# Block one's two attentions: one written-out order for TensorE, ACT and DVE, with grouped-query scores two pairs a step and weight splits two at a time

## The chip, the cores and the metric

The kernel runs on one core of a Trainium2 chip. The metric is the device time in microseconds (us) of one execution. TensorE (PE in the rows) does the matmuls and transposes; ACT (ScalarE), DVE (VectorE) and POOL (GpSimd) work beside it; SP (SyncE) issues the loads. Matmul results land in PSUM banks, from which ACT and DVE read them.

## The reference, cut to what matters

Two transformer blocks on x of 256 x 1024, all in float32. The change touches the first: its projections, two attentions, and the output projection. The feed-forward part of it, and the whole second block, follow.

```python
h = rmsnorm(x, attn_norm_g)
qa, ka, va, qb, kb, vb = split(h @ w_in)        # 512, 128, 128, 512, 512, 512 columns
# A: grouped-query, 8 query heads on 2 key/value heads of 64, rotary positions
qa, ka = rope(rmsnorm(qa, a_q_norm_g)), rope(rmsnorm(ka, a_k_norm_g))
out_a = softmax(qa @ ka.T * 64**-0.5) @ va
# B: differential, 4 heads, each with two query/key parts of 64 and values of 128
qb, kb = rmsnorm(qb, b_q_norm_g), rmsnorm(kb, b_k_norm_g)
p = softmax(qb @ kb.T * 64**-0.5 + rel_bias[t5_bucket(k_pos - q_pos)])   # for each part c = 0, 1
ob = (p[c=0] - lam * p[c=1]) @ vb
out_b = rmsnorm(ob, b_subln_g) * (1 - 0.2)
x = x + concat(out_a, out_b) @ w_out
u = relu(rmsnorm(x, mlp_norm_g) @ w_up) ** 2
x = x + u @ w_down
x = second_block(x, c, ...)                     # modulation c @ w_ada_2, two gated FFNs, two mixers
```

## The kernel before

**Products and their weights.** A float32 product is made of three matmuls on values split in a high and a low half (`block`, L265 to L267: high x high, high x low, low x high). The 256 rows are two tiles of 128, the index `t` (or `qt` for queries). Half a chunk of 512 output columns is one *block*: 12 matmuls of 128 x 512. Weights come through the class `Stream`: pieces of 512 KB are loaded by SP into a ring of seven `raw` buffers and split into `hi` and `lo` in a ring of six, or in places of their own (`wbig`, `wph`). One split is an ACT copy (L137) and a DVE subtraction (L138). `split_to(i)` writes the splits up to item `i` into the program; `need` does so for the items a chunk is about to read. Between the weights stand the pieces of `w_ada_2`, of which DVE makes the second block's modulation (`mod`, L487).

**Generators as filler.** `chunk` projects 512 columns: for each `t` half the blocks, a `yield`, the other half, then its evacuation. The evacuations of `kb` and `qb` (`ev_b`) are a head norm (ACT square, DVE reduction L456, ACT logarithm and exp, three DVE steps L251 to L253, the multiply L466 into `kn`), four transposes (L727), and an ACT copy into `kbT` or `qbT` (L728); transposes are put in the list `later`, which the next `flush()` empties. `vb` is copied by ACT (L735). The list `filler` holds these generators, and `fill(n)` runs n steps of it. `wout_q(t, kh)` is the output projection, one generator for each query tile and each attention (`kh` 0 is A, 1 is B).

**The attentions.** `gqa()` (A) and `diff()` (B) each return three stages. A unit of A is (`qt`, `jp`, `g`), a pair of query heads on one key head; at `g` 0 it issues the scores of both `g` into two `aux` banks. Its DVE work is a maximum (L769) and its product with the norm (L771), its ACT work two exps (L774), its ratio a reciprocal (L778). A unit of B is (`qt`, `hp`): eight matmuls (L827) into two `aux` banks, the bias added on DVE (L834), maxima (L838), four exps on ACT (L841), then reciprocal and combination on DVE (L844 to L849) into `s`. Stage two transposes (L785, L856) and copies the result to `eT` or `aT`; stage three multiplies with the values (L798, and its like for B) and, with the last unit of a query tile, normalises into `oa` or `ob` and transposes that to the operand `MX` of the output projection (`to_hl`, L389). There are three `acc`, four `aux` and one `flex` PSUM banks.

**What sets the order.** The units are interleaved by `ga_[:6] + df_[:3] + ga_[6:7] + df_[3:] + ga_[7:]`; each loop step runs the three stages of three neighbouring units and one `fill()`. PE runs in the order in which the code issues (`manual_schedule` for PE); the order of ACT and DVE in the same stretch is chosen by the tile scheduler. SP issues loads as ring buffers come free.

Of the kernel before, what the change touches and what calls it, by code (L numbers as in the profile page):

```python
# [15 lines left out]
ALU = mybir.AluOpType  # L16
# [4 lines left out]
P = 128  # L21
# [143 lines left out]
def body(ctx: ExitStack, tc: tile.TileContext, a: dict, out: bass.AP):  # L165
# [120 lines left out]
    def chunk(xv, items, n, evac, ahead=4):  # L286

        st.need(items)
        for t in range(2):
            ps = acc()  # L290
            if t == 0:
                st.split_to(items[-1] + 1 + ahead)
            half = (len(items) + 1) // 2
            block(ps, *xv, 0, items[:half], t, n, True, False)
            yield
            block(ps, *xv, 2 * half, items[half:], t, n, False, True)
            flush()
            evac(t, ps)
            yield
# [440 lines left out]

# [9 lines left out]
    def gqa():  # L750
        pv, rec, ex, exT, sc2 = {}, {}, {}, {}, {}

        def scores(u):
            qt, jp, g = u
            if jp == g == 0:
                rec[qt] = small(8, "rec")
            if g == 0:

                for w in range(2):
                    sc2[w] = aux()  # L760
                for i in range(2):
                    for w in range(2):
                        nc.tensor.matmul(
                            sc2[w][:, i * S : (i + 1) * S], qaT[w * 64 : (w + 1) * 64, 2 * jp + i, qt * P : (qt + 1) * P],
                            kaT[w * 64 : (w + 1) * 64, :], start=True, stop=True,
                        )
            ps = sc2.pop(g)
            nm, sm = small(2, "nm"), small(2, "sm")
            nc.vector.tensor_reduce(nm, ps.rearrange("p (g k) -> p g k", g=2), AX, ALU.max, negate=True)  # L769
            h = 4 * g + 2 * jp  # L770
            nc.vector.tensor_tensor(nm, nm, rq[:, qt, h : h + 2], ALU.mult)  # L771
            e = s512("e")
            for i in range(2):
                nc.scalar.activation(  # L774
                    e[:, i * S : (i + 1) * S], ps[:, i * S : (i + 1) * S], AF.Exp, bias=nm[:, i : i + 1],
                    scale=rq[:, qt, h + i : h + i + 1], accum_out=sm[:, i : i + 1],
                )
            nc.vector.reciprocal(rec[qt][:, h : h + 2], sm)  # L778
            ex[u] = e

        def trans(u):
            e = ex.pop(u)
            p2 = aux()
            for b in range(4):
                nc.tensor.transpose(p2[:, b * P : (b + 1) * P], e[:, b * P : (b + 1) * P], ident)  # L785
            eT = s512("eT")
            nc.scalar.activation(eT, p2, AF.Copy)
            exT[u] = eT

        def pvs(u):  # L790
            qt, jp, g = u
            if jp == g == 0:
                pv[qt] = acc()
            eT = exT.pop(u)
            for i in range(2):
                h = 4 * g + 2 * jp + i
                for kt in range(2):
                    nc.tensor.matmul(  # L798
                        pv[qt][:, h * 64 : (h + 1) * 64], eT[:, (2 * i + kt) * P : (2 * i + kt + 1) * P], va[:, kt, g * 64 : (g + 1) * 64],
                        start=kt == 0, stop=kt == 1,  # L800
                    )
            if jp == g == 1:
                oa = s512("oa")
                nc.vector.tensor_tensor(
                    oa.rearrange("p (h d) -> p h d", d=64), pv[qt].rearrange("p (h d) -> p h d", d=64),
                    rec[qt].unsqueeze(2).to_broadcast([P, 8, 64]), ALU.mult,
                )
                fill()
                to_hl(oa, MX, 0, qt)

        return scores, trans, pvs

    def diff():
        pv, at, atT, rec = {}, {}, {}, {}

        def scores(u):
            qt, hp = u
            flex_free[0] = False
            if hp == 0:
                rec[qt] = small(8, "recb")  # L820
            s = []
            nm, sm, rr = small(4, "nm"), small(4, "sm"), small(4, "rr")
# [8 lines left out]
            for c in range(2):  # L831
                ps = pss[c]
                s.append(s512("s"))
                nc.vector.tensor_tensor(  # L834
                    s[c].rearrange("p (h k) -> p h k", h=2), ps.rearrange("p (h k) -> p h k", h=2),
# [3 lines left out]
                for i in range(2):  # L839
# [3 lines left out]
                    )  # L843
            nc.vector.reciprocal(rr[:, 2:4], sm[:, 2:4])  # L844
# [4 lines left out]
            nc.vector.scalar_tensor_tensor(rec[qt][:, 2 * hp : 2 * hp + 2], sm[:, 0:2], EPS, sm[:, 0:2], ALU.mult, ALU.mult)  # L849
            at[u] = s[0]  # L850

        def trans(u):
            att = at.pop(u)
# [5 lines left out]
            atT[u] = aT  # L859

        def pvs(u):
            qt, hp = u
            if hp == 0:
                pv[qt] = bank("flex", 1)
            aT = atT.pop(u)
            for i in range(2):
                h = 2 * hp + i
                for kt in range(2):
                    nc.tensor.matmul(
                        pv[qt][:, h * P : (h + 1) * P], aT[:, (2 * i + kt) * P : (2 * i + kt + 1) * P], vb[:, kt, h * P : (h + 1) * P],  # L870
                        start=kt == 0, stop=kt == 1,
                    )
            if hp == 1:
                ob = s512("ob")
                head_norm(pv[qt], 4, P, ob, each=rec[qt])
# [649 lines left out]
```

## Time and profile before

| | |
|---|---|
| time, median of 3 runs | 1037.38 us (1036.73 to 1038.09) |
| the profiled execution: its time, its span | 1038.07 us, 1036.3 us |
| mean granted clock of PE over the span | 0.984 |
| PE busy | 997.0 us, 96% of the span, 5825 instructions |
| DVE busy | 724.8 us, 70% |
| ACT busy | 509.8 us, 49% |
| POOL busy | 23.2 us, 2% |
| DMA engines busy, of 16 | 61.9% (loads) |

Busy times are sums over one engine's instructions; the granted clock is the share of full speed that PE was allowed, 1.0 being 2.4 GHz and 0.5 being 1.2 GHz. A start in a row counts from the start of the span. A name such as `aux` or `kn` is a buffer of the program, `out<-in` what an instruction writes and reads.

### The profile page before, as it was taken

The numbers are of one execution on the slowest core, as the hardware profiler recorded it, in microseconds if no ns is written. First come the engines' busy times: TensorE is split into PE (matmuls) and PEld (weight loads), VectorE is DVE, ScalarE is ACT, GpSimd is POOL, SyncE is SP. The second block draws the span as 40 slices with busy tenths as digits, with TensorE's granted clock in tenths as the row PEclk, the third lists the DMA queues.
The fourth block names the chain that finished last, engine by engine and source line by source line (L and its number), as shares of the span: only waits on it lengthen the run. The fifth ranks groups of instructions, "written<-read, shape, count | busy, mean of one in ns | idle before, by whom it ended". The sixth has DMA issues, their size and how long they took to land.

```text
span 1036.3 us, 15123 instructions
## 1 busy us (share of the span) xinstructions
PE 997.0 (96%) x5825; PEld 863.0 (83%) x5825; DVE 724.8 (70%) x1006; ACT 509.8 (49%) x779; POOL 23.2 (2%) x38
## 2 busy tenths in 40 slices
PE   8788779999999999999999999999999989999998
PEld 7666567999888799998878987888887869999987
DVE  7857355789776577777855969977678776666652
ACT  6556245655455345444625566444373445444540
POOL 1000000000000100000010000000010000000000
PEclk8988899999999999999999999999999999999999
DMA  9745025788988188869924656766456636774741
GB/s 313 229 149 184 1 82 184 220 294 299 319 272 276 34 285 256 267 212 351 341 104 143 203 167 183 251 206 220 133 183 223 212 114 208 244 236 138 260 155 40
DMA packets 104714, 212.22 MB, mean 205 GB/s; under 512 B 7934, under 2 KB 15034, under 8 KB 104643
## 3 DMA queue, kind: packets, MB, share of 16 engines
q1 hardware_dynamic: 104642, 211.27, 61.9%
q8 instruction: 45, 0.74, 0.3%
q14 instruction: 27, 0.21, 0.1%
HBM read 209.14 MB, written 2.10 MB: 204 GB/s over the span
## 4 chain that ended last, share of the span: by engine, by line
PE 65%; issue 18%; DVE 2%; ACT 1%; POOL 0%; DVEq 0%; ACTq 0%; POOLq 0%
PE acc L265 9%; PE acc L267 9%; PE acc L266 9%; PE acc L325 7%; PE acc L327 7%; PE acc L326 7%; PE flex L267 3%; PE flex L265 3%; PE flex L266 3%; PE flex L325 2%; PE flex L326 2%; PE flex L327 2%; PE aux L389 1%; DVE lo L138 1%; PE aux L497 0%
## 5 line engine op out<-in xcount | busy, mean ns | idle before, releaser
L138 DVE TENSOR_TENSOR lo<-raw,hi 128x1024 fp32r<-128x1024 f32 (+1 forms) x297 | 349.2, 1185 | 121.7 <-ACT hi L137 120.3
L137 ACT ACTIVATE hi<-raw 128x1024 fp32r<-128x1024 f32 (+1 forms) x297 | 302.9, 1028 | 162.1 <-PE acc L267 69.9
L325 PE MATMUL acc<-X,hi 128*128 128x256 f32 x624 | 176.2, 282 | 0.0
L327 PE MATMUL acc<-X,hi 128*128 128x256 f32 x624 | 175.7, 282 | 0.0
L326 PE MATMUL acc<-X,lo 128*128 128x256 f32 x624 | 175.4, 281 | 0.0
L265 PE MATMUL acc<-hi,X 128*128 128x512 f32 (+1 forms) x336 | 135.1, 404 | 3.4 <-ACT X L393 1.2
L267 PE MATMUL acc<-hi,X 128*128 128x512 f32 (+1 forms) x336 | 132.7, 396 | 0.9 <-DVE X L394 0.9
L266 PE MATMUL acc<-lo,X 128*128 128x512 f32 (+1 forms) x336 | 132.9, 397 | 0.2 <-DVE lo L138 0.2
L325 PEld LDWEIGHTS acc<-X,hi 128*128 128x128 f32 x624 | 118.3, 190 | 0.3
L326 PEld LDWEIGHTS acc<-X,lo 128*128 128x128 f32 x624 | 118.2, 189 | 0.2
L327 PEld LDWEIGHTS acc<-X,hi 128*128 128x128 f32 x624 | 118.2, 189 | 0.1
L487 DVE SCALAR_TENSOR_TENSOR mod<-raw,sc,mod 128x1024 f32<-128x1024 f32 x72 | 91.9, 1277 | 0.1
L265 PEld LDWEIGHTS acc<-hi,X 128*128 128x128 f32 x336 | 64.7, 193 | 18.6 <-ACT X L393 2.6
L267 PEld LDWEIGHTS acc<-hi,X 128*128 128x128 f32 x336 | 64.7, 193 | 14.9 <-DVE X L394 1.7
L266 PEld LDWEIGHTS acc<-lo,X 128*128 128x128 f32 x336 | 64.7, 193 | 13.0 <-DVE lo L138 0.4
L267 PE MATMUL acc<-hi,U 128*128 128x512 f32 x174 | 68.5, 394 | 0.0
L266 PE MATMUL acc<-lo,U 128*128 128x512 f32 x174 | 68.3, 394 | 0.0
L265 PE MATMUL acc<-hi,U 128*128 128x512 f32 x174 | 68.1, 393 | 0.0
L325 PE MATMUL flex<-X,hi 128*128 128x256 f32 x208 | 58.7, 282 | 0.0
L327 PE MATMUL flex<-X,hi 128*128 128x256 f32 x208 | 58.5, 281 | 0.0
L326 PE MATMUL flex<-X,lo 128*128 128x256 f32 x208 | 58.5, 281 | 0.0
L325 PEld LDWEIGHTS flex<-X,hi 128*128 128x128 f32 x208 | 39.4, 190 | 0.1
(423 smaller groups left out, 1607.2 us busy)
## 6 DMA issues: line engine op xcount, KB each, us to landing
raw<-in_ffn_w_in_dram SPq DMA_DIRECT2D x80, 512.0 KB, 4.8
raw<-in_w_ada_dram SPq DMA_DIRECT2D x72, 512.0 KB, 5.3
raw<-in_w_mix_dram SPq DMA_DIRECT2D x64, 512.0 KB, 4.8
raw<-in_ffn_w_out_dram SPq DMA_DIRECT2D x44, 512.0 KB, 5.1
raw<-in_w_up_dram SPq DMA_DIRECT2D x32, 512.0 KB, 5.2
raw<-in_w_down_dram SPq DMA_DIRECT2D x32, 512.0 KB, 4.8
raw<-in_w_in_dram SPq DMA_DIRECT2D x16, 512.0 KB, 6.2
raw<-in_w_out_dram SPq DMA_DIRECT2D x16, 512.0 KB, 4.7
```

Of the source, the lines that this page charges most:

```text
L137: nc.scalar.activation(hi[:, :, :n], r[:, :, :n], AF.Copy)
L138: l = getattr(nc, eng).tensor_tensor(lo[:, :, :n], r[:, :, :n], hi[:, :, :n].bitcast(F32), ALU.subtract)
L265: nc.tensor.matmul(ps[:, c0:n], h, hi[:, j, c0:n], start=f, stop=False)
L266: nc.tensor.matmul(ps[:, c0:n], h, lo[:, j, c0:n], start=False, stop=False)
L267: nc.tensor.matmul(ps[:, c0:n], l, hi[:, j, c0:n], start=False, stop=z)
L325: nc.tensor.matmul(ps, h, xh, start=first, stop=False, skip_group_check=True)
L326: nc.tensor.matmul(ps, l, xh, start=False, stop=False, skip_group_check=True)
L327: nc.tensor.matmul(ps, h, xl, start=False, stop=last, skip_group_check=True)
L389: nc.tensor.transpose(ps[:, b * P : (b + 1) * P], src[:, b * P : (b + 1) * P], ident)
L487: nc.vector.scalar_tensor_tensor(v, r.rearrange("p a c -> p (a c)"), sc[:, k : k + 1], v, ALU.mult, ALU.add)
```

## The change

`gqa()` and `diff()` become the classes `Gqa` and `Diff`, whose stages are methods: `scores`, `ratios`, `trans`, `values`, `norm`, `out`. A unit of A is now (`qt`, `jp`): its scores, maxima and exps for both `g` come in one step, two head pairs at a time. The reciprocals move to `ratios`, which stands behind the step's filler; the multiply into `oa` or `ob` moves to `norm`, the transposes of it to `out`, a step later. Eight units in a fixed list, and a table of filler counts, replace `units`, `step`, `ready`, `named` and `have`. `chunk` with `even=True` and `wout_q` call `split_to` behind every block, and `wout_q` also `flush()`es; the end of `ev_wo` (the transposes of the new x) goes into `later`. `manual_schedule` covers ACT and DVE beside PE. The number of instructions of each kind is the same on every engine; POOL's order is the same too. The diff, cut:

```diff
-    def chunk(xv, items, n, evac, ahead=4):
+    def chunk(xv, items, n, evac, ahead=4, even=False):
+
 
         st.need(items)
         for t in range(2):
@@ -292,8 +293,12 @@
                 st.split_to(items[-1] + 1 + ahead)
             half = (len(items) + 1) // 2
             block(ps, *xv, 0, items[:half], t, n, True, False)
+            if even:
+                st.split_to(items[-1] + 1 + ahead)
             yield
             block(ps, *xv, 2 * half, items[half:], t, n, False, True)
+            if even:
+                st.split_to(items[-1] + 1 + ahead)
             flush()
...
+        def scores(self, u):
+            qt, jp = u
+            if jp == 0:
+                self.rec[qt] = small(8, "rec")
+
+            pss = [aux(), aux()]
+            for i in range(2):
+                for g in range(2):
+                    nc.tensor.matmul(
+                        pss[g][:, i * S : (i + 1) * S], qaT[g * 64 : (g + 1) * 64, 2 * jp + i, qt * P : (qt + 1) * P],
+                        kaT[g * 64 : (g + 1) * 64, :], start=True, stop=True,
+                    )
+            self.ex[u], self.sm[u] = [], []
+            for g in range(2):
+                ps, h = pss[g], 4 * g + 2 * jp
+                nm, sm = small(2, "nm"), small(2, "sm")
+                nc.vector.tensor_reduce(nm, ps.rearrange("p (g k) -> p g k", g=2), AX, ALU.max, negate=True)
+                nc.vector.tensor_tensor(nm, nm, rq[:, qt, h : h + 2], ALU.mult)
+                e = s512("e")
                 for i in range(2):
-                    for w in range(2):
+                    nc.scalar.activation(
+                        e[:, i * S : (i + 1) * S], ps[:, i * S : (i + 1) * S], AF.Exp, bias=nm[:, i : i + 1],
+                        scale=rq[:, qt, h + i : h + i + 1], accum_out=sm[:, i : i + 1],
+                    )
+                self.ex[u].append(e)
+                self.sm[u].append(sm)
...
+        def ratios(self, u):
+            qt, jp = u
+            for g, sm in enumerate(self.sm.pop(u)):
+                nc.vector.reciprocal(self.rec[qt][:, 4 * g + 2 * jp : 4 * g + 2 * jp + 2], sm)
...
             block(wo_ps[n, t], *mv, 4 * kh, it_wo[kh][n], t, 512, first, not first)
+            st.split_to(it_wo[1][1][-1] + 1)
+            flush()
             if not first:
                 ev_wo(n, t, wo_ps[n, t])
             yield
...
     def ev_wo(n, t, ps):
         ev_res(n, t, ps)
-        gained(t, n, R_GM, X)
-        if n == 1:
-            nc.vector.reciprocal(r2[:, t : t + 1], var_of(t))
-
-
-    gqa_stages, gqa_units = gqa(), [(qt, jp, g) for qt in range(2) for jp in range(2) for g in range(2)]
-    diff_stages, diff_units = diff(), [(qt, hp) for qt in range(2) for hp in range(2)]
-    ga_, df_ = [(gqa_stages, u, (), 0) for u in gqa_units], [(diff_stages, u, ("kb", "qb"), 1) for u in diff_units]
-    units = ga_[:6] + df_[:3] + ga_[6:7] + df_[3:] + ga_[7:]
-
-    def step(i, stages, u, needs, kh):
-        if i == 0:
-            have(*needs)
-        if i == 2 and kh == 1:
-            have("vb")
-        stages[i](u)
-        if i == 2 and all(u[1:]):
-            filler.append(wout_q(u[0], kh))
-
-
-    pe_order = ExitStack()
-    pe_order.enter_context(tc.manual_schedule(engines={mybir.EngineType.PE}))
+
+        def rest():
+            gained(t, n, R_GM, X)
+            if n == 1:
+                nc.vector.reciprocal(r2[:, t : t + 1], var_of(t))
+        later.append(rest)
+
+
+
+    order = ExitStack()
+    order.enter_context(tc.manual_schedule(engines={mybir.EngineType.PE, mybir.EngineType.Activation, mybir.EngineType.DVE}))
+    flex_free[0] = False
+    A, B = Gqa(), Diff()
+    units = [(A, 0, 0), (A, 0, 1), (A, 1, 0), (B, 0, 0), (B, 0, 1), (A, 1, 1), (B, 1, 0), (B, 1, 1)]
+    fills = [(1, 1), (1, 0), (1, 0), (1, 1), (1, 1), (0, 0), (0, 1), (0, 1), (0, 2), (0, 0), (0, 0)]
     fill(4)
     for qt in range(2):
         o = 255 - P * qt
         nc.sync.dma_start(bias[:, :, qt, :], tr[:, :, o : o + S])
-    for i in range(len(units) + 2):
-        for j in range(3):
-            if 0 <= i - j < len(units):
-                step(j, *units[i - j])
-        fill()
+    n = len(units)
+    for i in range(n + 3):
+        fill(fills[i][0])
+        ends = units[i - 3] if i >= 3 and units[i - 3][2] == 1 else None
+        if ends:
+            if i == n + 2:
+                fill()
+            ends[0].norm(ends[1])
+        if i < n:
+            units[i][0].scores(units[i][1:])
+        if 1 <= i <= n:
+            units[i - 1][0].trans(units[i - 1][1:])
+        if ends:
+            if i == n + 2:
+                fill()
+            ends[0].out(ends[1])
+            filler.append(wout_q(ends[1], 0 if ends[0] is A else 1))
+        fill(fills[i][1])
+        if i < n:
+            units[i][0].ratios(units[i][1:])
+        if 2 <= i <= n + 1:
+            units[i - 2][0].values(units[i - 2][1:])
     drain()
     flush()
-    pe_order.close()
+    order.close()
```

The stages not shown hold the instructions of the old ones. Three places show what moves. In the rows the number behind a name tells buffers apart (`raw_375` is the same load in both programs), and x2 means twice.

DVE at the norm of `kb`, tile 0, which ends with the multiply into `kn`; L138 rows are low halves of weight pieces, L251 to L253 with `rq` belong to the query norm. Before:

```order
L138 TENSOR_TENSOR lo_635<-raw_375,hi_634 128x1024
L251 SCALAR_TENSOR_TENSOR newton<-ms,e_188,rq 128x8
L456 TENSOR_REDUCE ms<-sq 128x8
L138 TENSOR_TENSOR lo_641<-raw_413,hi_640 128x1024
L252 SCALAR_TENSOR_TENSOR newton<-newton,rq 128x8
L138 TENSOR_TENSOR lo_648<-raw_419,hi_647 128x1024
L253 SCALAR_TENSOR_TENSOR rq<-newton,rq 128x8
L138 TENSOR_TENSOR lo_654<-raw_473,hi_653 128x1024
L251 SCALAR_TENSOR_TENSOR newton<-ms,e_188,rs 128x8
L252 SCALAR_TENSOR_TENSOR newton<-newton,rs 128x8
L253 SCALAR_TENSOR_TENSOR rs<-newton,rs 128x8
L466 TENSOR_TENSOR kn<-acc,rs 128x512
```

After (L461 and L471 are the old L456 and L466):

```order
L251 SCALAR_TENSOR_TENSOR newton<-ms,e_188,rq 128x8
L461 TENSOR_REDUCE ms<-sq 128x8
L252 SCALAR_TENSOR_TENSOR newton<-newton,rq 128x8
L253 SCALAR_TENSOR_TENSOR rq<-newton,rq 128x8
L251 SCALAR_TENSOR_TENSOR newton<-ms,e_188,rs 128x8
L252 SCALAR_TENSOR_TENSOR newton<-newton,rs 128x8
L253 SCALAR_TENSOR_TENSOR rs<-newton,rs 128x8
L471 TENSOR_TENSOR kn<-acc,rs 128x512
L138 TENSOR_TENSOR lo_587<-raw_375,hi_586 128x1024
L138 TENSOR_TENSOR lo_593<-raw_413,hi_592 128x1024
```

The norm now ends ahead of the splits instead of behind four of them.

ACT between the scores of A and the copies that end the projections: `eT` are copies of transposed exps, `s` the exps of B, `wbig`, `wph` and `hi` high halves of weight pieces (here of `w_out`), `qbT` the copy of the transposed query projection. Before:

```order
L774 ACTIVATE e,sm<-aux,nm,rq 128x256 x2
L787 ACTIVATE eT<-aux 128x512
L774 ACTIVATE e,sm<-aux,nm,rq 128x256 x2
L787 ACTIVATE eT<-aux 128x512
L735 ACTIVATE vb<-acc,r_187 128x512
L728 ACTIVATE qbT<-acc,gq_207 128x4x128
L393 ACTIVATE MX<-flex 128x4x128
```

After (L798 is the old L787, L733 the old L728, L740 the old L735, L852 the old L841):

```order
L798 ACTIVATE eT<-aux 128x512 x2
L137 ACTIVATE wbig<-raw_528 128x1024
L137 ACTIVATE wbig<-raw_590 128x1024
L137 ACTIVATE wph<-raw_596 128x1024
L137 ACTIVATE hi_864<-raw_636 128x1024
L852 ACTIVATE s,sm<-s,nm 128x256 x4
L798 ACTIVATE eT<-aux 128x512 x2
L733 ACTIVATE qbT<-acc,gq_207 128x4x128
L740 ACTIVATE vb<-acc,r_187 128x512
```

The copy into the last `qbT` now stands behind four high halves and the exps of a B unit.

DVE ahead of the transposes of B(1,0), the first B unit of query tile 1; `s` at the end is what they read, `rr` and `recb` the ratios. Before:

```order
L834 TENSOR_TENSOR s<-aux,bias 128x512 x2
L838 TENSOR_REDUCE nm<-s 128x2 x2
L849 SCALAR_TENSOR_TENSOR recb<-sm 128x2
L844 RECIPROCAL rr<-sm 128x2
L845 SCALAR_TENSOR_TENSOR rr<-rr,nlam,sm 128x2
L848 SCALAR_TENSOR_TENSOR s<-s,rr 128x256 x2
```

After (L860 to L865 are the old L844 to L849, L492 the old L487):

```order
L849 TENSOR_REDUCE nm<-s 128x2
L138 TENSOR_TENSOR lo_1104<-raw_727,hi_1103 128x1024
L138 TENSOR_TENSOR lo_1108<-raw_733,hi_1107 128x1024
L492 SCALAR_TENSOR_TENSOR mod_1111<-raw_642,sc,mod_1111 128x1024
L138 TENSOR_TENSOR lo_1122<-raw_852,hi_1121 128x1024
L138 TENSOR_TENSOR lo_1128<-raw_857,hi_1127 128x1024
L860 RECIPROCAL rr<-sm 128x2
L138 TENSOR_TENSOR lo_1393<-raw_868,hi_1392 128x1024
L861 SCALAR_TENSOR_TENSOR rr<-rr,nlam,sm 128x2
L864 SCALAR_TENSOR_TENSOR s<-s,rr 128x256 x2
```

Between the maxima and the ratios of this unit there now stand five low halves and one modulation step.

## Rows read from the trace of the kernel before

**Rows 1.** Windows: stretch, length, busy PE, PEld, DVE, ACT, POOL, PEclk, DMA, GB/s.

```profile
46.40:166.30 119.90, 95.71 (x480) 74.24 (x480) 66.00 (x127) 56.22 (x126) 3.01 (x4) 0.90 0.34 109
166.30:1036.30 870.00, 861.29 (x5158) 755.41 (x5156) 622.95 (x790) 424.57 (x597) 15.12 (x23) 1.00 0.65 214
```

**Rows 2.** Waits of PE, 46.4 to 166.3: waited for, total us, times, longest.

```profile
PE aux L389 <- DVE ob L466: 8.0, 2, 4.6
PE aux L856 <- DVE s L848: 5.1, 2, 4.8
PE acc L727 <- DVE kn L466: 3.8, 1, 3.8
PE aux L785 <- ACT e L774: 3.2, 1, 3.2
```

**Rows 3.** Timeline of PE: start us, length us, line, operation, out<-in.

```profile
46.03 0.40 PE L267 MATMUL acc<-hi,X 128*128 128x512 f32 x1
...
88.92 1.13 PE L827 MATMUL aux<-kbT,qbT 64*128 64x256 f32 x8
89.98 0.66 PE L785 MATMUL aux<-ident,e 128*128 128x128 f32 x4
90.48 1.00 PE L798 MATMUL acc<-va,eT 128*128 128x64 f32 x8
91.29 0.48 PE L265 MATMUL acc<-hi,X 128*128 128x512 f32 x1
...
94.26 1.13 PE L827 MATMUL aux<-kbT,qbT 64*128 64x256 f32 x8
...
151.13 0.48 PE L265 MATMUL acc<-hi,X 128*128 128x512 f32 x1
...
156.74 0.40 PE L265 MATMUL acc<-wbig,MX 128*128 128x512 f32 x1
...
181.28 0.28 PE L325 MATMUL acc<-X,hi 128*128 128x256 f32 x1
```

**Rows 4.** Timeline of PE behind two long waits: a block and what follows.

```profile
102.65 0.77 PE L265 MATMUL acc<-wbig,MX 128*128 128x512 f32 x1
...
106.75 1.13 PE L827 MATMUL aux<-kbT,qbT 64*128 64x256 f32 x8
...
142.52 0.65 PE L265 MATMUL acc<-hi,MX 128*128 128x512 f32 x1 [0.78 <-ACT MX L396]
...
147.00 1.00 PE L798 MATMUL acc<-va,eT 128*128 128x64 f32 x8
```

**Rows 5.** Timelines of DVE and of ACT; brackets: idle before, and its releaser.

```profile
65.70 0.69 DVE L456 TENSOR_REDUCE ms<-sq 128x8 f32<-128x512 f32 x1 [3.46 <-ACT sq L454]
66.56 0.69 DVE L769 TENSOR_REDUCE nm<-aux 128x2 f32<-128x512 f32 x1 [0.18 <-PE aux L763]
...
67.82 0.69 DVE L466 TENSOR_TENSOR kn<-acc,rs 128x512 f32<-128x512 f32 x1
...
71.53 2.36 DVE L138 TENSOR_TENSOR lo<-raw,hi 128x1024 fp32r<-128x1024 f32 x2 [0.78 <-ACT hi L137]
...
89.88 1.28 DVE L487 SCALAR_TENSOR_TENSOR mod<-raw,sc,mod 128x1024 f32<-128x1024 f32 x1
...
92.21 1.28 DVE L834 TENSOR_TENSOR s<-aux,bias 128x512 f32<-128x512 f32 x2
...
67.56 0.56 ACT L774 ACTIVATE e<-aux,nm,rq 128x256 f32<-128x256 f32 x1 [0.59 <-DVE nm L771]
68.66 0.59 ACT L787 ACTIVATE eT<-aux 128x512 f32<-128x512 f32 x1
...
76.95 2.01 ACT L137 ACTIVATE wbig<-raw 128x1024 fp32r<-128x1024 f32 x2
...
94.12 0.51 ACT L841 ACTIVATE s<-s,nm 128x256 f32<-128x256 f32 x1
```

**Rows 6.** Windows, one stretch of 5 us; columns as in rows 1.

```profile
135.00:140.00 5.00, 2.66 (x24) 2.42 (x22) 2.45 (x7) 2.85 (x8) 0.71 (x1) 1.00 0.00 0
```

More of the change, by code (lines that the diff above doesn't have):

```diff
@@ L772, in scores @@
[L772 to L807, printed above, removed]
-                fill()
-                to_hl(oa, MX, 0, qt)
@@ L811, in gqa, with norm @@
[L811 to L816, printed above, removed]
+                            self.pv[qt][:, h * 64 : (h + 1) * 64], eT[:, (2 * i + kt) * P : (2 * i + kt + 1) * P],
+                            va[:, kt, g * 64 : (g + 1) * 64], start=kt == 0, stop=kt == 1,
+                        )
+        def norm(self, qt):
+            self.oa[qt] = s512("oa")
+            nc.vector.tensor_tensor(
+                self.oa[qt].rearrange("p (h d) -> p h d", d=64), self.pv[qt].rearrange("p (h d) -> p h d", d=64),
+                self.rec[qt].unsqueeze(2).to_broadcast([P, 8, 64]), ALU.mult,
+            )
@@ L817, in scores, with out, __init__ @@
+        def out(self, qt):
+            to_hl(self.oa.pop(qt), MX, 0, qt)
+    class Diff:
+        def __init__(self):
+            self.pv, self.at, self.atT, self.rec, self.sm, self.rs, self.ob = {}, {}, {}, {}, {}, {}, {}
+        def scores(self, u):
             qt, hp = u
-            flex_free[0] = False
             if hp == 0:
-                rec[qt] = small(8, "recb")
+                self.rec[qt] = small(8, "recb")
             s = []
-            nm, sm, rr = small(4, "nm"), small(4, "sm"), small(4, "rr")
+            nm, sm = small(4, "nm"), small(4, "sm")
@@ L843, in scores, with ratios @@
                     )
+            self.at[u], self.sm[u] = s, sm
+        def ratios(self, u):
+            qt, hp = u
+            s, sm, rr = self.at[u], self.sm.pop(u), small(4, "rr")
             nc.vector.reciprocal(rr[:, 2:4], sm[:, 2:4])
@@ L858, in trans, with values @@
             nc.scalar.activation(aT, p2, AF.Copy)
-            atT[u] = aT
-        def pvs(u):
+            self.atT[u] = aT
+        def values(self, u):
             qt, hp = u
             if hp == 0:
-                pv[qt] = bank("flex", 1)
-            aT = atT.pop(u)
+                self.pv[qt] = bank("flex", 1)
+            aT = self.atT.pop(u)
             for i in range(2):
@@ L873, in pvs, with norm, out @@
             if hp == 1:
-                ob = s512("ob")
-                head_norm(pv[qt], 4, P, ob, each=rec[qt])
-                fill()
-                to_hl(ob, MX, 4, qt, g=gsub)
-        return scores, trans, pvs
+                self.rs[qt] = small(8, "rs")
+                head_norm(self.pv[qt], 4, P, None, each=self.rec[qt], r=self.rs[qt])
+        def norm(self, qt):
+            self.ob[qt] = s512("ob")
+            nc.vector.tensor_tensor(
+                self.ob[qt].rearrange("p (h d) -> p h d", d=P), self.pv[qt].rearrange("p (h d) -> p h d", d=P),
+                self.rs[qt][:, :4].unsqueeze(2).to_broadcast([P, 4, P]), ALU.mult,
+            )
+        def out(self, qt):
+            to_hl(self.ob.pop(qt), MX, 4, qt, g=gsub)
     evs = {"kb": ev_b(kbT, gbk), "qb": ev_b(qbT, gbq), "vb": ev_vb}
@@ L912, in body @@
     nc.vector.tensor_tensor(sc, sc, c8, ALU.mult)
-    ready = set()
-    def named(nm, xv):
-        yield from chunk(xv, it_c[nm], 512, evs[nm])
-        ready.add(nm)
     for nm in ("kb", "qb", "vb"):
-        filler.append(named(nm, xv))
-    def have(*nms):
-        if not ready.issuperset(nms):
-            while not ready.issuperset(nms):
-                fill()
-            flush()
+        filler.append(chunk(xv, it_c[nm], 512, evs[nm], even=True))
     wo_ps = {}
```

49 lines of the change are left out of this document (25 added, 24 removed).

## The prediction

> **What bounds the kernel now.** I read the busy times by stretch first. The attention part of block one and what shares it, 46.4 to 166.3 us, is the one long stretch in which TensorE (PE) is not full: busy 95.71 of 119.90, mean granted clock 0.90. After it PE is busy 861.29 of 870 at 1.00 [rows 1]. The instructions are the same in number and kind in both kernels, only their order changes, and PE's order from the second up-projection tile on does not. So what PE loses less in this stretch arrives at the end in full, and nothing else can be won. The waits of PE in the stretch name the losers: transposes that wait for DVE (`ob` 8.0, `s` 5.1, `kn` 3.8) and for ACT (`e` 3.2) [rows 2]; with the short ones 24.2 us (119.90 - 95.71). Then the clock: after each long wait PE runs for a while at 1.2 instead of 2.4 GHz. A block of 12 matmuls takes 2.97 with its hand-overs (91.29 to 94.26) [rows 3], but 4.10 and 4.48 behind such waits [rows 4], and the small pieces ahead of it double too. I take 2 us for each of five restarts: 10 us.
>
> **PE's own work.** Piece prices are distances between starts [rows 3]: a score step 1.06 (88.92 to 89.98), four transposes 0.50, the values of one unit 0.81, a block 2.97, or 2.80 in a run (24 matmuls of 151.13 to 156.74 in 5.61). From the end of the `kb` projection, 46.26 (46.03 and one pace of 0.23), to the first up matmul of the other form at 181.28 there stand 16 blocks (2.9 on average, 46.4), 96 up matmuls (8 run blocks, 22.4), 8 score steps 8.5, 12 units' transposes 6.0, 12 units' values 9.8 and 13 further sets of transposes (0.45, 5.9): 99.0 us of 135.0. Lost are 36.0: 24.2 waits, 10 clock, 1.8 unplaced gaps.
>
> **What the change does to the losses.** PE, ACT and DVE now run in the order written. I walked that order in time from 46.26, each instruction starting when its engine is free and its inputs are there. DVE: low half of a split 1.13 when back to back (two end after 2.36), reduction of a score tile to the start of its exp 1.0 (66.56 to 67.56), `s` add and its reduction 0.6 each (two adds in 1.28, exp at 94.12 after two adds and one reduction of 92.21 on), modulation 1.2. ACT: two exps 1.10 (67.56 to 68.66), those of `s` 0.5 each, copies 0.5, high half 0.97 (two in 2.01). A head norm takes 2.12 from its reduction to its last multiply (65.70 to 67.82) [rows 5]. (A is grouped-query, B differential; A(1,0) is query tile 1, step 0.)
>
> (a) *First norm.* DVE does the `kb` norm before the splits instead of among four. `kn` of tile 0 is there at 45.4, PE wants it at 46.3: the wait of 3.8 and its restart (2) go. What hides the splits now is the first `qb` half, split before. Zero.
>
> (b) *Third score step, A(1,0).* The ring of four `aux` banks hands it the banks of A(0,1), free when that step's exps have read them. DVE ends the second `kb` norm at 50.6, two low halves to 52.9, the reductions of A(0,0); ACT's exps end at 56.1, its copy and square at 57.2; the next norm, two reciprocals and two more low halves (2.26) hold DVE to 62.3; so exps of A(0,1) run 63.25 to 65.45. PE is there at 62. Wait 2.4, then 0.9 for the other bank: 3.3.
>
> (c) *B(0,0)* wants the banks of A(1,0) the same way: 72.2 and 73.3 against 71.7: 1.3.
>
> (d) *Second half of `vb`.* Its bank frees when ACT has copied the last `qbT`. Ahead of that copy on ACT stand four high halves of `w_out`, the exps of B(0,0) and two `eT`. ACT ends the exps of A(1,0) and two `eT` at 74.26; first high half 75.3; four low halves on DVE to 79.87 (4.52); add and reduction, exp from 81.25, second pair of exps to 83.45, two `eT` 84.4, copy 85.1. PE is through with A(0,1)'s values at 79.95. Wait 5.2, and a restart, 2: together 7.2. This is the largest wait that the change creates.
>
> (e) The exps of A(1,1) gate B(1,0)'s scores and the transposes after: 1.0.
>
> (f) *Transposes of B(1,0).* DVE reaches its ratios only behind five low halves and one modulation. ACT gives the first high half at 106.9, after the exps of B(1,0) and two `eT`; 5 x 1.13 + 1.2 + two small ones, 7.0, then the first half of the `s` update 0.7: 114.6. PE has nothing from 106.9 on: 7.7. The `ob` transposes behind it need the square, DVE's reduction, POOL's power and a multiply queued after that: 2.2 more. Restart: small pieces 1.0 and the block 2.0, so 3.
>
> (g) Tail: `oa` 0.4, the first up split 0.3, the second `ob` 0.4. The waits that [rows 2] shows for `ob` shrink here because output blocks stand between.
>
> Sum after: 3.3 + 1.3 + 7.2 + 1.0 + 7.7 + 2.2 + 3.0 + 1.1 = 26.8, and unplaced gaps between 0 and 1.8, where I take 1: 27.8. Gain 36.0 - 27.8 = 8.2. Against the profiled run that is span 1036.3 to 1028.1 (its time, 1038.07, is 1.77 above its span and 0.7 above the median); against the median 1037.38 it gives **1029.2**.
>
> Costed at nothing: the two score pairs a step (same matmuls; the second pair only comes earlier), splits two at a time outside (b), (d), (f) (under projection blocks), the later residual tail (ACT and DVE are free there, and output blocks cover it), the load order (up loads now behind `g_ml`, which waits for the last `w_out` tile in phase memory; the load behind it waits for a split of the same moment anyhow, and is needed 20 us later).
>
> **The clock, both ways.** Unknown is what waits of 2.4 (b), 1.3 (c) do to it. Low end: nothing, and the restarts at (d) and (f) cost nothing either, -5: 1024. High end: after (b) too, though of that PE's slack of 5.2 before (d) hides most, and 1.8 of gaps instead of 1, and ACT and DVE hand-overs 0.03 longer on some 60 steps: +5: 1034. In the kernel before, 135 to 140 us has PE busy only 2.66 of 5 in many short pieces, and the clock stays 1.00 [rows 6]; so I take no loss from short waits. The Trainium skill (TensorE: Matmul & The Clock Gate, "A second HAM failure mode: psum-queue depth-cycling") says otherwise: frequent micro-idles between matmul groups make the clock swing between its two levels. By that rule the sum would be the second rival's time; [rows 6] does not bear it out.
>
> **Rivals.** (1) *All waits filled.* If ACT and DVE kept ahead everywhere, PE would lose only gaps: 1037.38 - 34 = 1003. For it: PE's work is 99 of 135. Against: (b), (d), (f) are DVE and ACT queues with nothing to overtake. 3%.
> (2) *Slower: the lower clock holds from (b) to the output blocks.* Every step there has a wait. Half speed doubles PE's pieces: before (d) 9 us more against a slack of 5, so 4; from (d) to (f) 19 us of pieces, of which 2 are counted and 2 fall into waits, so 15; behind (f) 2 before the long run of blocks: +21, minus 3 of waits filled: 1047. It turns the sign once more than 8 us of PE's path is at the lower level beyond what I counted. Against it: every restart before recovers within one or two blocks [rows 4]. 6%.
> (3) *No change.* The four `w_out` pieces of (d) are loaded behind the two transfers of the bias; if they land 8 us after ACT wants the first (74.3), the whole gain sits in (d): 1037. For it: ACT now waits in order, with exps behind. Against: I put their issue at 50 to 53, over 20 us earlier. 6%.
> (4) The order does not bind: excluded for the three engines, since the built rows stand in it.
>
> **Chances.** Forecast 82%, rivals 3, 6 and 6, unnamed 3. The forecast's own bounds are 1024 and 1034, which with its edges leaves about 2 in 10 out. What can be told from no change is 0.2%, 2.1 us. Faster: 82 + 3 and half of the unnamed, 86%; same: 6 and a little, 7%; slower 7%.
>
> **What the profile after would show.** No wait at the first `kn` transposes near 46; PE waiting for ACT near 62 (`e`) 2 to 3 us; the longest waits near 80 (a `vb` projection matmul waiting for ACT's `qbT` copy, 5) and near 107 (B transposes waiting for DVE's `s`, 8, with five L138 ahead on DVE); two restarts, not five; the up stage 8 us earlier, PE full from there. Wrong would be: these two waits missing or twice as long, or a clock below 1.00 where PE only pauses for 1 to 2 us.

## The result and the profile after

The changed kernel takes **1027.34 us** (median of 4 runs, 1026.46 to 1029.29), the kernel before 1037.74 beside it; the ratio is 0.9903, 95% interval 0.9886 to 0.9920. 1029.2 was predicted, 1024 to 1034. The profiled execution took 1029.29 us with a span of 1027.5, against 1038.07 and 1036.3 before; the 8.8 us between the spans are compared here.

I measure the attention stretch from the transposes of the first `kn` (or, where they wait, from the moment TensorE is free for them) to the first up matmul of the other form. Before these are 46.26 and 181.28, 135.0 us apart [rows 3]; now 45.55 and 171.57. The windows view of after (stretch, length, busy PE, PEld, DVE, ACT, POOL, PEclk, DMA share, GB/s):

```profile
45.55:171.57 126.02, 109.57 (x550) 87.80 (x548) 74.90 (x132) 65.30 (x139) 3.01 (x4) 0.89 0.38 127
171.57:1027.50 855.93, 847.02 (x5089) 743.09 (x5087) 614.54 (x780) 414.66 (x585) 15.14 (x23) 0.99 0.64 214
```

So 9.0 us went in the stretch. It begins 0.7 earlier, as executions of the same beginning differ anyhow (44.7 in e3, 46.6 in e12, below), and the rest takes 0.9 longer (1036.3 - 181.28 = 855.0 before): that nearly cancels. The waits of PE from 46.4 to 166.3 that answer to [rows 2] (engine, line, what was waited for: total us, times, longest):

```profile
PE aux L871 <- DVE s L864: 7.8, 1, 7.8
PE acc L265 <- ACT qbT L733: 2.9, 1, 2.9
PE aux L767 <- ACT e L779: 2.7, 2, 2.3
PE aux L394 <- DVE ob L894: 2.1, 1, 2.1
PE aux L394 <- DVE oa L816: 0.3, 1, 0.3
PE acc L266 <- DVE lo L138: 0.3, 1, 0.3
PE aux L839 <- ACT e L779: 0.2, 1, 0.2
```

16.3 us instead of 24.2. `kn` is gone, `ob` fell from 8.0 to 2.1, the short waits for x and `MX` are gone; `s`, now another step's, rose from 5.1 to 7.8. The places, in the timeline of PE (start, length, operation; in brackets the idle time before it and its releaser):

```profile
45.55 0.60 PE L732 MATMUL acc<-ident,kn 128*128 128x128 f32 x4
...
63.77 0.70 PE L767 MATMUL aux<-kaT,qaT 64*128 64x256 f32 x2 [2.28 <-ACT e L779]
64.86 1.13 PE L767 MATMUL aux<-kaT,qaT 64*128 64x256 f32 x6 [0.40 <-ACT e L779]
...
84.78 0.80 PE L265 MATMUL acc<-hi,X 128*128 128x512 f32 x1 [2.94 <-ACT qbT L733]
...
115.28 1.09 PE L871 MATMUL aux<-ident,s 128*128 128x128 f32 x4 [7.85 <-DVE s L864]
118.43 1.08 PE L394 MATMUL aux<-ident,ob 128*128 128x128 f32 x4 [2.06 <-DVE ob L894]
119.17 0.77 PE L265 MATMUL acc<-wph,MX 128*128 128x512 f32 x1
```

What held the last `qbT` copy, in the timeline of ACT: four high halves of `w_out`, a wait of 3.24 us for the maxima of B(0,0), which DVE makes behind the low halves of the same pieces, then the exps of B(0,0), two `eT` and the copy:

```profile
73.62 2.03 ACT L137 ACTIVATE wbig<-raw 128x1024 fp32r<-128x1024 f32 x2
75.51 1.08 ACT L137 ACTIVATE wph<-raw 128x1024 fp32r<-128x1024 f32 x1
76.46 1.08 ACT L137 ACTIVATE hi<-raw 128x1024 fp32r<-128x1024 f32 x1
80.78 0.51 ACT L852 ACTIVATE s<-s,nm 128x256 f32<-128x256 f32 x1 [3.24 <-DVE nm L849]
...
83.10 1.06 ACT L798 ACTIVATE eT<-aux 128x512 f32<-128x512 f32 x2
84.05 0.68 ACT L733 ACTIVATE qbT<-acc,gq 128x512 f32<-128x512 f32 x1
```

And what held the ratios of B(1,0), in the timeline of DVE: two low halves, a modulation, three low halves, and only then the update of `s`:

```profile
107.46 2.36 DVE L138 TENSOR_TENSOR lo<-raw,hi 128x1024 fp32r<-128x1024 f32 x2 [3.13 <-ACT hi L137]
109.74 1.28 DVE L492 SCALAR_TENSOR_TENSOR mod<-raw,sc,mod 128x1024 f32<-128x1024 f32 x1
110.94 2.35 DVE L138 TENSOR_TENSOR lo<-raw,hi 128x1024 fp32r<-128x1024 f32 x2
...
113.28 1.20 DVE L138 TENSOR_TENSOR lo<-raw,hi 128x1024 fp32r<-128x1024 f32 x1
...
114.65 0.88 DVE L864 SCALAR_TENSOR_TENSOR s<-s,rr 128x256 f32<-128x256 f32 x2
```

### The profile page after: what moved, and what is told of

It is laid out like the page before. It is cut to its first block, busy times and chain, and to the rows that moved or that the text cites. A ratio compares the mean times of both kernels' runs of the same rounds, so it can differ in the third digit from the quotient of the medians.

```text
span 1027.5 us, 15148 instructions
## 1 busy us (share of the span) xinstructions
PE 995.6 (97%) x5825; PEld 863.4 (84%) x5825; DVE 725.5 (71%) x1006; ACT 507.9 (49%) x779; POOL 23.2 (2%) x38
## 4 chain that ended last, share of the span: by engine, by line
PE 88%; DVE 6%; ACT 3%; issue 2%; DMA 1%; SPq 0%; POOL 0%; ACTq 0%; DVEq 0%; POOLq 0%
PE acc L265 14%; PE acc L267 14%; PE acc L266 14%; PE acc L330 7%; PE acc L332 7%; PE acc L331 7%; PE flex L267 4%; PE flex L265 3%; PE flex L266 3%; PE flex L330 2%; PE flex L331 2%; PE flex L332 2%; DVE lo L138 2%; PE aux L394 1%; PE aux L1406 1%
## 5 line engine op out<-in xcount | busy, mean ns | idle before, releaser
L138 DVE TENSOR_TENSOR lo<-raw,hi 128x1024 fp32r<-128x1024 f32 (+1 forms) x297 | 348.4, 1184 | 124.9 <-ACT hi L137 123.2
L330 PEld LDWEIGHTS acc<-X,hi 128*128 128x128 f32 x624 | 117.6, 188 | 0.3
L492 DVE SCALAR_TENSOR_TENSOR mod<-raw,sc,mod 128x1024 f32<-128x1024 f32 x72 | 91.9, 1277 | 0.1
L138 DVE TENSOR_TENSOR wbig<-raw,wbig 128x1024 fp32r<-128x1024 f32 x22 | 26.7, 1223 | 19.3 <-ACT wbig L137 19.0
```

The costliest lines, as they stand in the source:

```text
L138: l = getattr(nc, eng).tensor_tensor(lo[:, :, :n], r[:, :, :n], hi[:, :, :n].bitcast(F32), ALU.subtract)
L330: nc.tensor.matmul(ps, h, xh, start=first, stop=False, skip_group_check=True)
L492: nc.vector.scalar_tensor_tensor(v, r.rearrange("p a c -> p (a c)"), sc[:, k : k + 1], v, ALU.mult, ALU.add)
```

## The experiments

Executions of one kernel lie 0.6 to 7.9 us apart, so medians are compared as ratios to the kernel before in the same batch (its medians there: 1039.0 to 1039.6). "Against after" is (ratio - 0.9903) x 1039; its interval is about 2.5 us to either side. The stretch is that of the profiled execution, which is the slowest of its kernel for after, e7 and e12 and the fastest for e2, e3 and e15.

| run | median us | ratio, 95% interval | against after | stretch us |
|---|---|---|---|---|
| before | 1037.7 | 1 | +10 | 135.0 |
| after | 1027.3 | 0.9903 (0.9886 to 0.9920) | 0 | 126.0 |
| e1 after, order kept on PE alone | 1026.9 | 0.9885 (0.9860 to 0.9910) | -1.9 | 122.1 |
| e7 before, order kept on ACT and DVE | 1050.8 | 1.0123 (1.0098 to 1.0149) | +22.9 | 148.7 |
| e13 after, `norm` and `out` at once | 1036.4 | 0.9970 (0.9958 to 0.9981) | +7.0 | 134.5 |
| e12 after, residual's tail at once | 1030.4 | 0.9919 (0.9905 to 0.9933) | +1.7 | 129.4 |
| e2 after, first `w_out` splits later | 1027.1 | 0.9891 (0.9868 to 0.9913) | -1.2 | 119.9 |
| e3 after, ratios of B(1,0) first | 1025.5 | 0.9873 (0.9854 to 0.9893) | -3.1 | 122.1 |
| e5 after, `qb`'s splits later | 1027.9 | 0.9897 (0.9878 to 0.9915) | -0.6 | 124.6 |
| e9 after, other `w_out` splits spread | 1023.6 | 0.9845 (0.9823 to 0.9866) | -6.0 | 122.2 |
| e10 e9 and e2 | 1021.9 | 0.9832 (0.9808 to 0.9856) | -7.4 | 119.0 |
| e11 e10, low halves behind the maxima | 1013.2 | 0.9755 (0.9737 to 0.9773) | -15.4 | 111.5 |
| e14 e11, blocks into the last two waits | 1012.3 | 0.9738 (0.9725 to 0.9750) | -17.1 | 110.1 |
| e15 e14, order kept on PE alone | 1022.7 | 0.9849 (0.9833 to 0.9865) | -5.6 | 117.6 |

**What is keeping an order worth?** e1 frees ACT and DVE in the changed kernel, e7 binds them in the kernel before.

```diff
-    order.enter_context(tc.manual_schedule(engines={mybir.EngineType.PE, mybir.EngineType.Activation, mybir.EngineType.DVE}))
+    order.enter_context(tc.manual_schedule(engines={mybir.EngineType.PE}))
```

> The changed kernel with TensorE alone kept in the written order; ACT and DVE are again ordered by the scheduler. In the built rows the first `kn` stands behind four low halves again, the low halves of the second half of `w_out` are spread over the B units, and none stands ahead of the ratios of B(1,0). Theory 1 (each place gains or loses by what stands ahead of it in its queue): the wait for `kn` near 46 us is back (about 4 us and a restart of 2), most of the wait for `s` near 107 (7.9) and its restart are gone; in all 1015 to 1028 us, I take 1020, below the changed kernel's 1027.3. Theory 2 (the gain of 10 us is the kept order on ACT and DVE as such): back to 1035 to 1039.

Its waits of PE:

```profile
PE acc L732 <- DVE kn L471: 6.1, 2, 3.8
PE aux L871 <- DVE s L864: 2.9, 1, 2.9
```

Theory 2 falls: the time is that of the changed kernel within the intervals. Both halves of theory 1 are in the rows, `kn` back with the 3.8 of [rows 2], `s` down from 7.8 to 2.9; the time lies at the upper end of what was expected.

```diff
-    pe_order.enter_context(tc.manual_schedule(engines={mybir.EngineType.PE}))
+    pe_order.enter_context(tc.manual_schedule(engines={mybir.EngineType.PE, mybir.EngineType.Activation, mybir.EngineType.DVE}))
```

> The kernel before with one edit: ACT and DVE are kept in the order written too, as in the changed kernel, but units, stages and splits are the old ones. Here the first `kn` stands ahead of the splits, but each reciprocal stands right behind its own exps, so that DVE waits for ACT in every step, and four low halves stand behind the first of them. Theory 1 (an order is worth what stands in it; keeping it is worth nothing by itself): the wait for `kn` goes and longer ones come, 1038 to 1055, I take 1045. Theory 2 (keeping ACT and DVE in order is what gains): 1027 to 1031.

1.2% slower: theory 1. In its timeline of DVE (the first three rows) the first reciprocal waits for the exps, with four low halves queued behind it, and the second one waits likewise. PE now waits 7.1 us in three for high halves, which ACT makes in its own fixed order (last row, from its waits of PE):

```profile
52.43 0.17 DVE L778 RECIPROCAL rec<-sm 128x2 f32<-128x2 f32 x1 [1.33 <-ACT e L774]
53.37 4.63 DVE L138 TENSOR_TENSOR lo<-raw,hi 128x1024 fp32r<-128x1024 f32 x4 [0.78 <-DMA bias<-toep]
...
60.13 0.17 DVE L778 RECIPROCAL rec<-sm 128x2 f32<-128x2 f32 x1 [1.33 <-ACT e L774]
...
PE acc L265 <- ACT hi L137: 7.1, 3, 4.9
```

**Which part of the new order gains?** e13 takes back the step between the last values and their transposes.

```diff
-        ends = units[i - 3] if i >= 3 and units[i - 3][2] == 1 else None
+        ends = units[i - 2] if i >= 2 and i <= n + 1 and units[i - 2][2] == 1 else None
...
             units[i - 2][0].values(units[i - 2][1:])
+        if ends:
+            ends[0].norm(ends[1])
+            ends[0].out(ends[1])
+            filler.append(wout_q(ends[1], 0 if ends[0] is A else 1))
```

> The changed kernel with norm and transposes of `oa` and `ob` directly behind the last values, as before, without a step between. Theory 1 (the step between is what hides the chain of square, reduction, power and multiply): the wait for the last `ob` is back (about 4.6 us and a restart of 2 to 3), the other three are partly hidden in the waits of that place: 1034 (1031 to 1038). Theory 2 (those chains are hidden by output blocks anyway): 1026 to 1029.

Theory 1: 7.0 of the 10 us are lost again. In its timeline of PE the first `ob` takes over the wait of `s` and is longer, and the second has its own again, as [rows 2] had one of 4.6:

```profile
117.34 1.12 PE L394 MATMUL aux<-ident,ob 128*128 128x128 f32 x4 [11.98 <-DVE ob L894]
...
141.57 1.11 PE L394 MATMUL aux<-ident,ob 128*128 128x128 f32 x4 [4.96 <-DVE ob L894]
```

e12 takes back the later tail of the residual.

```diff
-        later.append(rest)
+        rest()
```

> The changed kernel with the end of each output block (the transposes of the new x) issued at once again, as before, instead of behind the next block. Theory 1 (the later tail is part of the gain): the waits of the transposes for x are back, 2.4 us in three, too short for the clock: 1029.7 (1028.5 to 1031). Theory 2 (the tail is covered by what else waits there): 1026.5 to 1028.

The waits for x are back in its waits of PE:

```profile
PE aux L446 <- DVE x L958: 1.6, 2, 0.8
PE acc L266 <- DVE lo L138: 1.1, 2, 0.8
```

With the 0.8 that the wait for `lo` has grown by, that is the 2.4 us of theory 1; the time rose by 1.7, and the intervals overlap, so the rows carry this verdict more than the times.

**The waits that the change makes, one by one.** e2 moves the four first `w_out` splits behind the first `vb` tile.

```diff
-            if t == 0:
+            if t == 0 and not late:
                 st.split_to(items[-1] + 1 + ahead)
...
-            if even:
+            if even and t >= late:
                 st.split_to(items[-1] + 1 + ahead)
...
-        filler.append(chunk(xv, it_c[nm], 512, evs[nm], even=True))
+        filler.append(chunk(xv, it_c[nm], 512, evs[nm], even=True, late=nm == "vb"))
```

> The changed kernel with the four high and low halves of the first `w_out` pieces moved from ahead of the `vb` projection to its second tile. Theory 1 (the wait of 2.9 us at the third `vb` half is made by these four on ACT and DVE, ahead of the exps of B(0,0) and the `qbT` copy): that wait goes to under 0.5 and its restart (2.5) with it, at most 1 us of new wait at the transposes of B(0,1), in whose queue the four now stand: 1022.5 (1021 to 1024.5). Theory 2 (the `qbT` copy is late by its own chain of norm, transposes and exps): the wait stays within 1 us and the time at 1026 to 1028.

The wait for `qbT` is gone from its waits of PE, so the four splits made it. But `oa`, now behind the moved low halves, waits 1.5 us, the longer of two:

```profile
PE aux L871 <- DVE s L864: 8.1, 2, 7.9
PE aux L394 <- DVE oa L816: 1.8, 2, 1.5
```

The time did not fall as expected. Its profiled execution took 1023.30 us, its other three 1026.72 to 1027.81. In the profiled one the clock stayed at 2.4 GHz behind the wait near 62 (windows view, PEclk third from the end):

```profile
63.16:72.20 9.04, 8.10 (x46) 6.05 (x46) 3.93 (x12) 5.91 (x19) 0.00 (x0) 1.00 0.16 57
```

For the other three only the mean granted clock of the whole execution is known: 0.985, 0.985 and 0.983, against 0.987 in the profiled one. So their clock was lower somewhere, which fits a fall behind this wait; the place is not shown.

e3 makes the ratios of B(1,0) ahead of the five low halves.

```diff
+        early = i in (6,)
+        if early:
+            units[i][0].ratios(units[i][1:])
         fill(fills[i][1])
-        if i < n:
+        if i < n and not early:
             units[i][0].ratios(units[i][1:])
```

> The changed kernel with one edit: the ratios of B(1,0) are issued ahead of the filler of their step, so that DVE makes them before the five low halves. Theory 1 (the five splits gate two chains, the ratios on DVE and the square for the norm of `ob` on ACT and DVE, and the second ends only 3 us later): the wait for `s` goes from 7.8 to under 0.5 us, the wait for `ob` grows from 2.1 to between 8 and 10, and the time falls by about 1 us, 1026.3 (1025 to 1028). Theory 2 (the place of the ratios is what costs): both waits and the restart go, 1015 to 1018.

Theory 1, in its waits of PE: the whole wait passes to `ob`, whose square stands behind the high halves on ACT and whose reduction behind the low halves on DVE.

```profile
PE aux L394 <- DVE ob L894: 9.2, 1, 9.2
```

e5 moves both pairs of splits that `qb` issues half a chunk on: for `qb` alone the calls of its first and third half go to the start of the second and the fourth.

```diff
-            if t == 0:
+            if t == 0 and not shift:
                 st.split_to(items[-1] + 1 + ahead)
...
-            if even:
+            if even and not shift:
                 st.split_to(items[-1] + 1 + ahead)
             yield
+            if shift:
+                st.split_to(items[-1] + 1 + ahead)
             block(ps, *xv, 2 * half, items[half:], t, n, False, True)
```

> The changed kernel with the two pairs of splits that the `qb` projection issues made one half chunk later, behind the maxima of A(0,0) and A(0,1) instead of ahead of them. Theory 1 (from 60 to 85 us the chain through ACT and DVE sets the time, and what TensorE loses near 62 in waiting, 2.7, and in clock, 4.0, is hidden in the later waits): the wait near 62 goes, the wait near 82 for `qbT` (2.9) grows by 5 or more, and the time falls by less than 1.5 us, 1026.7 (1025.5 to 1028). Theory 2 (TensorE's own time is what counts there): all 6.7 us are won, 1020.5 (1019 to 1022).

The time stays, as theory 1 has it, and the wait near 62 goes down to 0.4. But it doesn't reappear at `qbT`, as I expected: it stops at B(0,0), one step on, with the clock down behind it. The second half of `vb` starts 38.99 us behind the first `kn` transposes (84.98 - 45.99), in the changed kernel 39.23 (84.78 - 45.55): clearing the earlier wait has hardly moved it.

```profile
PE aux L841 <- ACT e L781: 2.5, 2, 2.3
PE acc L265 <- ACT qbT L735: 2.2, 1, 2.2
```

**A version with the queues cleared.** e9 spreads the five splits of the wait for `s`; in the loop the ratios of steps 6 and 7 go ahead of the filler as in e3, and the last splits behind `norm`.

```diff
-            st.split_to(it_wo[1][1][-1] + 1)
+            st.split_to((it_wo[1][0][n] if t == kh == 0 else it_wo[1][1][-1]) + 1)
...
+        if i == n:
+            st.split_to(it_wo[1][1][-1] + 1)
```

> The changed kernel with the splits of the second half of `w_out` spread: one behind the ratios of B(1,0), one behind those of B(1,1), the rest behind the norm of A's second query tile; the ratios of both B units ahead of the filler. Theory 1 (five low halves and five high halves ahead of ratios and square make the 12 us between 107 and 119): no wait for `s`, a wait for `ob` of 3 to 4 us (its own chain of square, reduction, power and multiply), a wait for `oa` under 1.5: about 8.7 us won, 1018.5 (1016.5 to 1021). Theory 2 (the splits then come too late for the output blocks, or `ob` is late anyhow): 1024 to 1028.

Its waits of PE:

```profile
PE aux L394 <- DVE ob L894: 3.5, 1, 3.5
PE aux L394 <- DVE oa L816: 2.6, 1, 2.6
```

The mechanism holds, `s` is gone and `ob` is at its own chain. The time does not: 1023.6 lies between the two ranges and in neither, a gain of 6.0 instead of 8.7. `oa`, behind a low half and a modulation, took 2.6 instead of under 1.5, and the clock fell behind it too (its four transposes took 1.12 us, at 2.4 GHz 0.66).

e10 adds the edit of e2 (and `norm` of A's first tile ahead of the filler).

> The kernel of e9 with the edit of e2 too (the four first `w_out` pieces split at the second tile of `vb`), and the norm of A's first query tile ahead of that half. Theory 1 (what the trace of e2 showed, 5 to 6 us less up to the transposes of B(1,0), holds and adds up): 1013 (1010.5 to 1016). Theory 2 (the times of e2, equal to those of the changed kernel, hold: TensorE's clock takes back what the wait gave): within 1.5 us of e9.

Theory 2, 1.4 us below e9. No wait for `qbT` is left (one of 1.7 for `s` has come), and the clock is down behind the wait near 62 (windows view; 0.51 is 1.2 GHz):

```profile
63.88:73.00 9.12, 9.12 (x34) 7.42 (x35) 4.00 (x13) 5.99 (x19) 0.00 (x0) 0.51 0.13 50
```

From those scores to the end of the next block e10 takes 12.1 us (63.88 to 75.97); e2, with the same instructions at the full clock, took 7.8 (63.16 to 70.96).

e11 removes that wait: in `split_to` the low halves of the two pairs go into a list, which the loop empties behind the scores and maxima of the unit; their high halves stay where they were.

```diff
+                if self.hold is None:
+                    low()
+                else:
+                    self.hold.append(low)
...
+        for low in st.hold or ():
+            low()
+        st.hold = [] if i == 0 else None
```

> The kernel of e10 with the low halves of the two pairs that `qb` splits held back on DVE until the maxima of A(0,0) and of A(0,1) are issued; their high halves stay where they are on ACT. Theory 1 (the maxima of A(0,0) and with them the whole chain through ACT and DVE up to the exps of A(1,0) come 2.3 to 4 us earlier, since the square for the next norm waits for no further high half): no wait near 62, under 1 us at B(0,0), 1008.5 (1005 to 1012). Theory 2 (the wait moves on, as it did in e5): within 1.5 us of e10.

Theory 1, and with 8 us below e10 the largest gain behind that of the change itself; the time is 1.2 above the range. The maxima of A(0,1) start 11.8 us behind the first `kn` transposes (57.21 - 45.42) instead of 16.0 in e10 (61.65 - 45.63). TensorE no longer waits near 62 and keeps its clock: from these scores to the end of the next block it takes 6.6 us (61.30 to 67.94), in e10 12.1 and ahead of them the wait of 2.3. The waits of PE that are left, and these scores in its timeline:

```profile
PE aux L401 <- DVE ob L901: 3.5, 1, 3.5
PE aux L401 <- DVE oa L823: 2.6, 1, 2.6
PE aux L878 <- DVE s L871: 1.3, 1, 1.3
...
61.30 1.14 PE L774 MATMUL aux<-kaT,qaT 64*128 64x256 f32 x8
```

e14 puts an output block ahead of the transposes of `ob` and of `oa`, the first two of these waits, and `norm` of B's first tile behind the scores of B(1,1).

```diff
-            if i == n + 2:
+            if i == n + 2 or i in (7, 8):
                 fill()
             ends[0].out(ends[1])
```

> The kernel of e11 with one output block moved into each of its two longest waits: ahead of the transposes of `ob` of the first query tile (wait 3.5 us there) and of `oa` of the second (2.6), and the adds of B(1,1) ahead of the `ob` multiply on DVE. Theory 1 (the blocks cover the two chains): both waits under 1 us, the restarts behind them gone: 1006 (1003.5 to 1009). Theory 2 (the ratios of B(1,1) or the high and low halves of `w_out` become late instead): within 2 us of the 1013.2 of e11.

Theory 2. `oa` waits no more, but DVE now does the adds and maxima of B(1,1) ahead of the `ob` multiply, and the ratios behind a low half and a modulation:

```profile
PE aux L878 <- DVE s L871: 3.6, 2, 2.3
PE aux L401 <- DVE ob L901: 2.1, 1, 2.1
```

It is the fastest kernel measured, 2.6% below the one before; from e11 it can't be told apart. e15 is e14 with PE alone kept in order.

> The kernel of e14 with TensorE alone kept in the written order; ACT and DVE ordered by the scheduler, which puts `kn` behind four low halves again. Theory 1 (here the written order holds no long queue any more, so what the scheduler changes only costs): the waits for `kn` (6.1 us in two) and their restarts (about 4) come on top: 1017 (1013 to 1022). Theory 2 (keeping the order on ACT and DVE is worth nothing in either kernel, as between the changed kernel and e1): within 1.5 us of e14.

Theory 1: 11.5 us slower than e14, the waits for `kn` first among its waits of PE. The expected range was missed by 0.7.

```profile
PE acc L739 <- DVE kn L478: 6.9, 2, 3.8
```

## Why the prediction was right, step by step

The stretch was to lose 27.8 us beside TensorE's own 99.0; in the profiled execution, 2.0 us above the median, it lost 126.0 - 99.0 = 27.0. (One term of the 99.0 is off by 0.1: twelve times 0.81 is 9.7, not 9.8.) The sum came out, but neither of its halves did: waits were to be 21.8 and were 16.3, clock and gaps 6 and were 10.7. In part the one error makes the other. The clock that fell at (b) cost 3.2, and 2.5 of that came off the waits that follow: e12, where it did not fall, waits 0.6 longer at (c) and 1.9 longer at (d). That the rest, 3.0 of waits too many and 2.2 of clock and gaps too few, nearly cancels is luck.

- **(a)** Right: the first `kn` transposes wait for nothing. e1 shows that the row's place in DVE's queue does it.
- **(b)** The wait was right, 2.7 against 3.3. The clock behind it was not: I took nothing, and 10.95 us passed from 63.77 to 74.72 at a mean of 0.69, where e2 needed 7.8: 3.2 lost. The reading behind that nothing was wrong. In the stretch of [rows 6] TensorE does not pause between many short pieces: it is busy without a break to 137.66 and then stands in one wait, 3.42 for `ob`, and the block at 142.52, which follows, ran mostly at 1.2 GHz (4.48 [rows 4]). So that row says nothing of what short waits do to the clock, for or against. The high end of the range had named this loss, and that the slack ahead of (d) would hide most of it.
- **(c)** 1.3 was forecast, nothing came, since TensorE was late by then (0.6 in e12).
- **(d)** The place, the queue and the end were right: 84.78 against 85.1. The wait was 2.9 instead of 5.2, because TensorE came 1.9 later. e12 runs the same program up to here, and there the clock did not fall behind (b): its wait is 4.84, and its block starts 39.28 us after its own `kn` transposes (85.88 - 46.60), in the changed kernel 39.23 (84.78 - 45.55); so it is in e3 (wait 1.37, 39.22) and e9 (3.53, 39.26). The chain through DVE and ACT sets this moment; what TensorE loses before it is swallowed. The restart was 2.5 (a block of 5.42 instead of 2.9), not 2.
- **(e)** 0.2 instead of 1.0.
- **(f)** Right: 7.85 against 7.7 for `s`, 2.06 against 2.2 for `ob`, and for the restart 3.2 against 3 (a block of 5.24 instead of 2.9, the transposes 0.9 longer). That the five high and low halves make both, and that `ob` would stand there without the first, e3 and e9 show.
- **(g)** 0.6 against 1.1.

The rows of [rows 6] in the timeline of PE before, for (b):

```profile
136.60 1.06 PE L869 MATMUL flex<-vb,aT 128*128 128x128 f32 x8
141.08 0.66 PE L389 MATMUL aux<-ident,ob 128*128 128x128 f32 x4 [3.42 <-DVE ob L466]
```

The row of e12's timeline of PE for (d):

```profile
85.88 0.79 PE L265 MATMUL acc<-hi,X 128*128 128x512 f32 x1 [4.84 <-ACT qbT L733]
```

The clock at (b) and (d), from the windows view of the changed kernel:

```profile
63.77:74.72 10.95, 10.55 (x44) 8.71 (x44) 4.09 (x13) 7.83 (x22) 0.00 (x0) 0.69 0.11 40
84.78:90.20 5.42, 5.42 (x12) 3.80 (x12) 0.45 (x1) 0.53 (x1) 0.00 (x0) 0.50 0.02 8
```

So there were three restarts, not the two that I had named as a sign. Of the rivals, (1) is refuted by the three waits; (2) began as told, with the lower clock from (b) on, but it was back before the next block was through (mean 0.69, not 0.5, in the first row above); (3) falls because ACT starts its first `w_out` high half at 73.62, right behind `eT`: the loads were there.

What the prediction did not tell is where the gain comes from. It walked the whole order, so its sum needed no answer; but it opened with ACT and DVE kept in order and gave the largest part half a sentence, that the waits for `ob` shrink because other work stands between. Undone alone, that step costs 7.0 of the 10 us (e13). Keeping the order on ACT and DVE gained nothing measurable in the changed kernel (e1), cost 1.2% in the one before (e7), and was worth 11.5 us in the kernel whose queues had been cleared (e14, e15). The parts don't add up, since each uncovers or hides the waits of the others.

Open stays what the unprofiled executions of e2, e9 and e10 lost. All three were expected 5 to 9 us lower by their waits, and e9 and e10 show the lower clock in their profiles. The mean granted clock of the other executions explains some of it and not all: in e10 the fastest (1017.0) has 0.995 and the slowest (1023.8) 0.985, but in e9 two that lie 2.4 us apart (1021.2 and 1023.6) have the same 0.992.

## What to carry to other kernels

Where several engines are kept in a written order, read each queue for what stands ahead of the step that TensorE waits for next: work with a distant deadline, such as weight splits, belongs behind it, half by half if one engine is free and the other is not (e11). Put a step of other work between the last product of a unit and the transposes that need its norm (e13). A wait that ends on a chain of other engines hides what TensorE loses before it, so that removing a loss ahead of it pays only when the chain gets shorter too (e5 and e12 against e11).

## What the chip showed beyond that

Behind one and the same wait near 62 us, 2.27 to 2.32 us and mostly a second of 0.40, the clock fell in five profiled executions (the changed kernel, e3, e9, e10, e13) and stayed at 2.4 GHz in two (e2, above, and e12, below, in the windows view). TensorE had done the same work before it in all seven. One of the two:

```profile
64.85:74.00 9.15, 8.17 (x48) 6.13 (x48) 4.04 (x13) 6.02 (x19) 0.00 (x0) 1.00 0.14 54
```

From those scores to the end of the next block the two took 7.80, the five between 10.36 (e9) and 12.52 (e3). That is 2.6 to 4.7 us, which a kernel pays or not depending on whether a later wait hides it. I had counted restarts as certain behind 5 us and as absent behind 2.4; at this length both occur.
